# The low half of a split weight tile: 4,096 bytes behind its high half in place of 4,224

## The chip, the cores and the metric

The kernel runs on one core of a Trainium2 chip. Its time is device time in microseconds of one execution. Three runs of the kernel before took 1101.42, 1101.83 and 1102.53 us; the median, 1101.83 us, is what the changed kernel's median is set against.

## The reference

One layer of a hybrid encoder on 256 positions of 2,048 channels, float32 throughout. Cut to the products that carry the time:

```python
hn = rmsnorm(h, mix_norm_pre)
proj = hn @ w_in                       # 2048 -> 1024 (z) + 1536 (xbc) + 32 (dt) + 1024 (u)
y_ssd = ssd_mixer(z, xbc, dt_raw, ...) # convolution, two chunked scans, gate, norm
y_pool = pool_mixer(u, pool_w, pool_scale)
h = h + rmsnorm(concatenate([y_ssd, y_pool]) @ w_out, mix_norm_post)   # 2048 -> 2048
hn = rmsnorm(h, ffn_norm_pre)
gate, val = split(hn @ w_ffn_up)       # 2048 -> 2 x 5632
ff = (gelu(dwconv_centred(gate, ...)) * val) @ w_ffn_down              # 5632 -> 2048
h = h + rmsnorm(ff, ffn_norm_post)
gate = sigmoid(rmsnorm(h, ple_norm_pre) @ w_ple_gate)                  # 2048 -> 2048
h = h + rmsnorm(gate * (p @ w_ple), ple_norm_post)                     # 256 -> 2048
```

## The kernel before, in words

**Split operands.** TensorE multiplies in a rounded 32-bit format (float32r). To keep float32 accuracy every operand is held as a high half, the value rounded to that format, and a low half, the rounded remainder. A product x w is then three matmuls: high x with high w, high x with low w, low x with high w. `split` makes the two halves of a weight: ScalarE copies the raw tile into the high half (line 195), VectorE subtracts that from the raw tile into the low half (line 196).

**Where the halves lie.** `weight_pair` takes one tile of 2,112 float32 columns (8,448 bytes in each partition) from a ring of five, and gives its first 1,056 columns to the high half and the rest to the low one. Only the first product, dtu, has 1,056 columns to a tile; all other weights come in pieces of 1,024 or 512 columns, which begin at the start of each half. Some weight tiles of the gate product do not come from the ring: they are given pages (tiles of 8,192 bytes, tag "pg"; names gth, gtl, gtfh, gtfl), high and low in pages of their own. Activations (hn, wox, cath, catl, dnxh, dnxl) lie in pages too; the split parts of the hidden layer (hs, hd) lie in tiles of 1,024 columns, high in front, low 512 columns behind.

**Three kinds of product use a weight tile.**

- `seven_products` and, for the output projection, `units` with `products`: two blocks of rows at once by a scheme of seven block products in place of eight. Tiles named a, b, c and d hold sums of weight blocks. For each block product the weight is the moving operand, 512 columns, in the order xh wh, xh wl, xl wh, into one bank: 21 matmuls for a unit (lines 341 and 1076). The lists WO_FAST (2 and 4 units), dn_fast (19 and 16) and gt_fast (3 and 3) say which units go this way.
- `token_major` and `units` otherwise: the weight is again the moving operand, 512 columns; for one stationary operand there are two matmuls, to two banks, and the order is xh wh twice, xh wl twice, xl wh twice (lines 398 and 1138). z, part of the output projection (woa), of the down product (dna), of the gate product (gt) and the embedding (ple) are done so.
- `feature_pairs`: the weight is the stationary operand, 128 columns, and the activation moves. For each weight slice there is a matmul of the high weights with 512 columns (high and low activation side by side) and one of the low weights with 256 (lines 414 and 415). xbc and the up projection (ga, va) are done so.

The stages follow each other: dtu up to 51 us, xbc to 136, z to 190, the output projection to 280, the up projection from 286 to 778, the down product to about 1003, the gate product to 1091. Weights stream in from HBM through queues of SyncE; block sums of weights are written back to HBM by GpSimd's queue and read again. The order of the instructions on ScalarE, VectorE and SyncE is recorded as it is written (`in_order`) and kept.

Of the kernel before, what the change touches and what calls it, by code (L numbers as in the profile page):

```python
# [86 lines left out]
def build(nc, a, out):  # L87
# [6 lines left out]
    with tile.TileContext(nc) as tc, \  # L94
# [82 lines left out]

        def weight_pair(name):
            w = wp.tile([P, 2112], F32R, tag="w", bufs=5, name=f"{name}w")
            return w[:, :1056], w[:, 1056:]  # L180

        def split(name, src, nel, cuts=()):

            if name in ready:
                return ready.pop(name)
            if name in spare:
                hi, lo = spare.pop(name)
            else:
                hi, lo = weight_pair(name)
            for c0, c1 in zip((0, *cuts), (*cuts, nel)):  # L190
                s = slice(c0, c1)
                v = src[:, s] if name != "dtu0" else r0[:, W_0[c0 // 352]:W_0[c0 // 352] + 352]
                if (name, c0) == ("dtu0", 0):
                    continue
                last["act"] = ins(nc.scalar.copy(hi[:, s], v))
                last["dve"] = ins(nc.vector.tensor_sub(lo[:, s], v, hi[:, s].bitcast(F32)))
            return hi, lo
# [279 lines left out]
        def first_panel(t):  # L477
            c = (V_SCW, W_0[1] - P)[t]
            return put([v[:, t * P:(t + 1) * P] for v in hn(0)], r0[:, c:c + P], r0[:, V_MIX:V_MIX + 1])

        spare["dtu0"] = weight_pair("dtu0")
        turned = ins(nc.vector.tensor_copy(spare["dtu0"][0][:, :352], r0[:, W_0[0]:W_0[0] + 352]))
        with tc.issue_after(turned):
# [870 lines left out]
        for i, w_ in enumerate(which[2:] + which[:2]):  # L1354
            fetch, add, store = block_sums(*w_, i >= len(which) - 2)
            n = 45 * i // 10 + 4
# [379 lines left out]
```

## Time and profile before

| | before |
|---|---|
| median of 3 runs | 1101.83 us (1101.42 to 1102.53) |
| the profiled execution's own time | 1101.12 us |
| its span, first to last instruction | 1099.3 us |
| mean granted TensorE clock | 0.999 |
| TensorE busy | 1093.2 us, 99% |
| VectorE busy | 976.7 us, 89% |
| ScalarE busy | 738.3 us, 67% |
| HBM traffic | 343 GB/s over the span |

Times in the profile's rows are microseconds, durations of one instruction nanoseconds. A row of the groups reads: line, engine, operation, written tile, read tiles, shape, count, then busy time and mean duration of one, then the engine's idle time before them and what ended it. A row of the timeline gives the start, the time taken and the engine, then the same; instructions of one kind that follow each other are merged, with their number behind the x. For a matmul the first of the tiles read that comes from a weight tile carries its name (dn_0w, gt08bw); the row does not say whether the high or the low half was read, so this is taken from the order in the code. The ends of matmuls are modelled; their starts are not.

### The profile page before, as it was taken

To read this page: it belongs to the slowest core of one execution; us is meant where nothing else is said; L and a number is where in the kernel's file an instruction comes from. 1 tells how busy PE (TensorE), PEld (TensorE's weight loads), DVE (VectorE), ACT (ScalarE), POOL (GpSimd) and SP (SyncE) were. 2 spreads that over 40 slices of the span, in tenths; PEclk is the share of its full clock that TensorE was granted. 3 is DMA by queue.
4 is the path that set the end of the run, shared out by engine and by line. 5 is a ranking of instruction groups with operands and counts; after the bars stand their busy time and mean duration, and the time that the engine had idled before them with its cause. 6 is when DMAs were issued, how large, how long until landed. Compare 5 with 4: busy or idle time off the path is not lost.

```text
span 1099.3 us, 15720 instructions
## 1 busy us (share of the span) xinstructions
PE 1093.2 (99%) x5766; PEld 936.8 (85%) x5766; DVE 976.7 (89%) x1367; ACT 738.3 (67%) x1109; POOL 98.8 (9%) x163
## 2 busy tenths in 40 slices
PE   9999999999999999999999999999999999999998
PEld 9988888888888888888888888888888888888886
DVE  6679988999879888889889988888999999999997
ACT  6687777566775565565756646657688878776773
POOL 0211101100100000000000000000000000051001
PEclk9999999999999999999999999999999999999999
DMA  9987699587589999999999998999999999995872
GB/s 361 423 253 208 193 273 277 211 323 267 186 343 402 395 403 368 393 360 364 385 370 379 366 391 346 401 364 421 356 411 382 370 350 385 418 380 226 312 276 77
DMA packets 59565, 367.45 MB, mean 334 GB/s; under 512 B 6672, under 2 KB 7696, under 8 KB 24208
## 3 DMA queue, kind: packets, MB, share of 16 engines
q1 hardware_dynamic: 45808, 302.74, 70.4%
q0 software_dynamic: 13536, 63.44, 17.3%
q8 instruction: 45, 0.74, 0.2%
q14 instruction: 32, 0.26, 0.1%
q10 hardware_dynamic: 144, 0.26, 0.1%
HBM read 315.56 MB, written 61.34 MB: 343 GB/s over the span
## 4 chain that ended last, share of the span: by engine, by line
PE 97%; DVE 1%; POOL 1%; ACT 0%; issue 0%; POOLq 0%; DVEq 0%; ACTq 0%
PE ga L123 22%; PE va L123 22%; PE dna L123 11%; PE xbc L123 6%; PE woa L123 5%; PE gt L123 5%; PE dns L123 4%; PE dtu L123 4%; PE z L123 4%; PE dn0s L123 2%; PE dn1s L123 2%; PE ple L123 1%; PE wo1s L123 1%; PE gts L123 1%; PE yd L123 1%; PE pw L123 1%
## 5 line engine op out<-in xcount | busy, mean ns | idle before, releaser
L123 PE MATMUL ga<-wox,ug_0w 128*128 128x512 f32 x704 | 130.8, 337 | 0.0
L123 PE MATMUL ga<-wox,ug_1w 128*128 128x512 f32 x704 | 130.1, 337 | 0.0
L123 PE MATMUL va<-wox,uv_1w 128*128 128x512 f32 x704 | 129.2, 337 | 0.0
L123 PE MATMUL va<-wox,uv_0w 128*128 128x512 f32 x704 | 129.2, 337 | 0.0
L123 PEld LDWEIGHTS ga<-wox,ug_0w 128*128 128x128 f32 x704 | 107.6, 188 | 14.5 <-ACT pl L1288 0.2
L123 PEld LDWEIGHTS va<-wox,uv_1w 128*128 128x128 f32 x704 | 107.5, 188 | 14.5
L123 PEld LDWEIGHTS va<-wox,uv_0w 128*128 128x128 f32 x704 | 107.5, 188 | 14.5
L123 PEld LDWEIGHTS ga<-wox,ug_1w 128*128 128x128 f32 x704 | 107.5, 188 | 14.5 <-DVE wox L233 0.2
L304 DVE TENSOR_TENSOR dnb<-dnb 128x512 f32<-128x512 f32 x128 | 88.2, 689 | 3.0
L282 POOL DMA_DIRECT2D dns<-dnb x30 | 16.1, 536 | 317.1 <-DVE dnb L304 266.0
L1205 ACT CAST he<-he 128x512 fp32r<-128x512 f32 x13 | 8.1, 621 | 42.7 <-DVE he L1204 42.7
L123 PE MATMUL xbc<-hn,xb_1w 128*128 128x512 f32 x192 | 36.5, 338 | 0.0
L123 PE MATMUL xbc<-hn,xb_0w 128*128 128x512 f32 (+1 forms) x192 | 36.5, 340 | 0.0
L123 PEld LDWEIGHTS xbc<-hn,xb_0w 128*128 128x128 f32 x192 | 29.7, 188 | 4.1
L123 PEld LDWEIGHTS xbc<-hn,xb_1w 128*128 128x128 f32 x192 | 29.5, 188 | 4.1 <-issue 0.2
L1368 ACT CAST hs<-hid 128x384 fp32r<-128x384 f32 (+1 forms) x44 | 23.4, 537 | 13.6 <-PE dna L123 13.4
L1448 ACT ACTIVATE fc<-gr,vt 128x256 f32<-128x256 f32 x44 | 26.1, 593 | 9.0 <-DVE gr L1441 9.0
L1520 POOL DMA_DIRECT2D hd<-hsum x24 | 12.7, 529 | 193.0 <-PE dn0s L123 70.5
L123 PE MATMUL dna<-dn_0w,hs 128*128 128x512 f32 x108 | 28.6, 394 | 0.0
L123 PE MATMUL dna<-dn_1w,hs 128*128 128x512 f32 x108 | 28.2, 392 | 0.0
L1369 DVE TENSOR_TENSOR hs<-hid,hs 128x384 fp32r<-128x384 f32 (+1 forms) x44 | 25.4, 580 | 2.6 <-ACT hs L1368 2.6
L1451 DVE TENSOR_TENSOR fc<-fc,ft 128x510 f32<-128x510 f32 x22 | 15.1, 689 | 11.3 <-ACT ft L1449 11.3
(1778 smaller groups left out, 2796.8 us busy)
## 6 DMA issues: line engine op xcount, KB each, us to landing
dnb<-w_down SPq DMA_DIRECT2D x32, 1024.0 KB, 10.6
dns<-dnb POOLq DMA_DIRECT2D x30, 1024.0 KB, 7.6
hd<-hsum POOLq DMA_DIRECT2D x24, 512.0 KB, 8.3
dtur<-w_dtu SPq DMA_DIRECT2D x14, 528.0 KB, 9.8
hsum<-he POOLq DMA_DIRECT2D x13, 512.0 KB, 8.0
gtb<-w_gate SPq DMA_DIRECT2D x6, 1024.0 KB, 10.5
gts<-gtb POOLq DMA_DIRECT2D x6, 1024.0 KB, 9.5
dn1r<-w_down SPq DMA_DIRECT2D x6, 1024.0 KB, 7.8
```

What stands on the lines that cost most here:

```text
L123: last["pe"] = ins(nc.tensor.matmul(o, lhsT, rhs, start=start, stop=stop, skip_group_check=True))
L282: nc.gpsimd.dma_start(t, pg[0])
L304: nc.vector.tensor_add(s[:, i], v[:, i], a[:, b])
L1205: nc.scalar.copy(o[:, :512], s[:, :512])
L1368: nc.scalar.copy(t[:, :c1], hid_part(k)[:, :c1])
L1369: nc.vector.tensor_sub(t[:, 512:512 + c1], hid_part(k)[:, :c1], t[:, :c1].bitcast(F32))
L1448: nc.scalar.activation(c[:, f], v[:, f], AF.Identity, bias=vec(V_FCB + 4 * s + 2 * i + f), scale=vec(w + NF))
L1451: nc.vector.tensor_add(c[:, :, 1:], c[:, :, 1:], l[:, :, :L - 1])
L1520: nc.gpsimd.dma_start(o.bitcast(F32), kept[k])
```

## The change

The high half keeps its place. The low half begins right behind the 1,024th column, 4,096 bytes behind the high half's start, and the tile's last 64 columns stay empty. Tiles of the first product (names that begin with dtu) keep 1,056 columns to a half, 4,224 bytes. The tile's size, the ring and all other tiles are as before, and so are the number, the kind and the order of the instructions on every engine.

```diff
         def weight_pair(name):
             w = wp.tile([P, 2112], F32R, tag="w", bufs=5, name=f"{name}w")
-            return w[:, :1056], w[:, 1056:]
+            n = 1056 if name.startswith("dtu") else 1024
+            return w[:, :n], w[:, n:2 * n]
```

## The prediction

> **What bounds the kernel now.** I read the page first: busy time per engine, then the chain that ended last.
>
> ```profile
> span 1099.3 us, 15720 instructions
> PE 1093.2 (99%) x5766; PEld 936.8 (85%) x5766; DVE 976.7 (89%) x1367; ACT 738.3 (67%) x1109; POOL 98.8 (9%) x163
> PE 97%; DVE 1%; POOL 1%; ACT 0%; issue 0%; POOLq 0%; DVEq 0%; ACTq 0%
> ```
>
> TensorE is busy 99% of the span and is 97% of the chain. What it waits for is almost nothing: the view of waits for PE holds two rows.
>
> ```profile
> PE dtu L140 <- DVE ones L138: 1.0, 1, 1.0
> PE mx L123 <- DVE mixl L767: 0.2, 1, 0.2
> ```
>
> So the time is the number of matmuls times the distance from one matmul's start to the next. A matmul's listed duration is modelled and overlaps the next one's; the distance is not in the groups, but the timeline gives starts, and a merged row's start less the start before it, divided by the matmuls between, is the spacing. The question of this case is whether the spacing depends on where an operand lies.
>
> The change moves no instruction: order and number are the same on all five engines, and every tile keeps its address. Tiles of the page, hs and weight pools all begin at remainder 96 when the address is divided by 256 (as the built program places them), and a slice of 512 columns is 2,048 bytes long, a multiple of 256. So in the products that carry the time every moving operand has remainder 96, except one kind: a low half 4,224 = 16 x 256 + 128 bytes behind its high half, remainder 224. The change gives it 4,096 = 16 x 256, remainder 96 like the rest.
>
> **Part 1, the seven-product units** (line 123, called from line 341 and, for the output projection, from line 1076; xh with wh, xh with wl, xl with wh, so every third moving operand is a low half). TensorE's timeline in the gate product:
>
> ```profile
> 1029.18 0.62 PE L123 MATMUL gt<-gt08bw,dnxh 128*128 128x512 f32 x2
> 1029.64 0.39 PE L123 MATMUL gt<-gt08bw,dnxl 128*128 128x512 f32 x1
> 1029.87 0.62 PE L123 MATMUL gt<-gt08dw,dnxh 128*128 128x512 f32 x2
> ...
> 1038.79 0.62 PE L123 MATMUL gt<-gt012bw,dnxh 128*128 128x512 f32 x2
> ```
>
> From 1029.18 to 1038.79 lie two units, 42 matmuls, in 9.61 us: 228.8 ns each. Inside a triple, high and low together take 0.46 us and the third matmul 0.23. The same order of three, with weights that lie in two page tiles (high and low both at remainder 96), stands later in the same product:
>
> ```profile
> 1068.35 0.39 PE L123 MATMUL gt<-gth,dnxh 128*128 128x512 f32 x1
> 1068.57 0.39 PE L123 MATMUL gt<-gtl,dnxh 128*128 128x512 f32 x1
> 1068.80 0.39 PE L123 MATMUL gt<-gth,dnxl 128*128 128x512 f32 x1
> ...
> 1071.07 0.69 PE L123 MATMUL gt<-gth,dnxh 128*128 128x512 f32 x2
> ```
>
> Twelve matmuls in 2.72 us: 226.7 ns each, the low ones 0.23 like the others. Two units at that spacing would be 42 x 0.2267 = 9.52 us, so a unit is 0.045 us too long, 6.4 ns for each of its seven low halves. The code has 47 such units (lists WO_FAST with 2 + 4, dn_fast with 19 + 16, gt_fast with 3 + 3): 47 x 0.045 = **2.1 us**. Is it load, not place, since few other engines work at 1068? In the busy down product the unit is the same:
>
> ```profile
> 822.65 0.85 PE L123 MATMUL dna<-dn018bw,hs 128*128 128x512 f32 x3
> 827.46 0.85 PE L123 MATMUL dna<-dn020bw,hs 128*128 128x512 f32 x3
> ```
>
> 21 matmuls in 4.81 us, 229.0 ns each. What costs the 6.4 ns, remainder 224 itself or the jump from 96 to 224 and back, makes no difference to the sum, since the change ends both.
>
> **Part 2, the regular products** (lines 398 and 1138: pairs of matmuls to two banks share a stationary operand; two of six move a low half).
>
> ```profile
> 1018.83 1.08 PE L123 MATMUL gt<-gt_0w,dnxh 128*128 128x512 f32 x4
> 1027.11 1.08 PE L123 MATMUL gt<-gt_1w,dnxh 128*128 128x512 f32 x4
> ```
>
> Here 36 matmuls took 8.28 us: 230.0 ns, 3.3 above the aligned 226.7. How many there are:
>
> ```profile
> L123 PE MATMUL dna<-dn_0w,hs 128*128 128x512 f32 x108 | 28.6, 394 | 0.0
> L123 PE MATMUL z<-z_1w,hn 128*128 128x512 f32 x96 | 24.6, 394 | 0.0
> L123 PE MATMUL woa<-wo_0w,cath 128*128 128x512 f32 x80 | 22.5, 395 | 0.0
> L123 PE MATMUL woa<-wo_0w,catl 128*128 128x512 f32 x40 | 13.5, 395 | 0.0
> L123 PE MATMUL gt<-gt_0w,dnxh 128*128 128x512 f32 x52 | 15.2, 392 | 0.0
> ```
>
> The 394 here is the modelled duration, not the spacing; only the counts are used. With the tiles of the other number: dna 216, z 192, woa 240, gt 104 and half as many again with dnxl, 156. The embedding's 48 I leave out. Whether all 3.3 ns go is open, since an aligned stretch just after an interruption is slow too:
>
> ```profile
> 1073.05 0.39 PE L123 MATMUL gt<-gth,dnxh 128*128 128x512 f32 x1
> 1073.97 0.39 PE L123 MATMUL gt<-gtl,dnxh 128*128 128x512 f32 x1
> ```
>
> Four in 0.92 us, 230.0 ns with nothing at 224. The bounds are therefore nothing and (216 + 192 + 240 + 156) x 3.3 = 2.7 us. I take all of it in dna and gt, 372 x 3.3 = 1.2 us, which run long without other matmuls between, and a third in z and woa, which are broken up by the mixer's small ones: 432 x 3.3 / 3 = 0.5. Together **1.7 us**.
>
> **Part 3, the feature products** (lines 414 and 415, xbc and the up projection), the longest stage. Here the weight tiles are stationary; the moving operand is a page, at 96 always. What moves is the load of the low weights.
>
> ```profile
> 600.48 2.94 PE L123 MATMUL ga<-wox,ug_0w 128*128 128x512 f32 x16
> 603.26 2.94 PE L123 MATMUL ga<-wox,ug_1w 128*128 128x512 f32 x16
> 606.03 2.94 PE L123 MATMUL ga<-wox,ug_0w 128*128 128x512 f32 x16
> ```
>
> From 600.48 to 606.03 lie 32 matmuls, 16 of 512 and 16 of 256 columns, in 5.55 us: 346.9 ns a pair. The first product, which the change leaves as it is, reads thirds of 352 columns:
>
> ```profile
> 39.72 3.05 PE L123 MATMUL dtu<-dtu12w,hn 128*128 128x352 f32 x18
> 42.60 3.05 PE L123 MATMUL dtu<-dtu13w,hn 128*128 128x352 f32 x18
> ```
>
> 18 in 2.88 us, 160.0 ns. With the aligned 226.7 at 512 that is a slope of 66.7 / 160 = 0.417 ns a column and 13.3 ns a matmul; a pair of 512 and 256 is then 226.7 + 120.0 = 346.7. The pairs are at it. Nothing is lost here, so nothing can come back: **0**, with a bound of 0.2 ns x 1,600 pairs (1,408 of the up projection, 192 of xbc, by the code's loops) = 0.3 us faster. The loss is priced under the rivals.
>
> The Trainium skill, "TensorE: Matmul & The Clock Gate", sections "Step-by-step: what each phase is for" and "Back-to-back issue gap", gives TensorE two independent read ports and a spacing of N / 2.4 + 2.5 ns, 215.8 ns at 512 columns, with no term for an address. By it the sum of this change would be zero. The trace disagrees with the figure (226.7 at best) and, by the two stretches of part 1, with there being no such term.
>
> **Part 4, the engines that fill the tiles.** Lines 195 and 196 write the two halves.
>
> ```profile
> L196 DVE TENSOR_TENSOR dn_1w<-dn1r,dn_1w 128x1024 fp32r<-128x1024 f32 x6 | 7.3, 1215 | 0.0
> L196 DVE TENSOR_TENSOR gtl<-gt1r,gth 128x1024 fp32r<-128x1024 f32 x4 | 4.8, 1218 | 0.0
> L195 ACT CAST dn_1w<-dn1r 128x1024 fp32r<-128x1024 f32 x6 | 6.3, 1052 | 2.8 <-PE dna L123 2.8
> L195 ACT CAST gth<-gt1r 128x1024 fp32r<-128x1024 f32 x4 | 4.0, 1054 | 0.0
> ```
>
> With both halves at 96 (gth, gtl) they take 3 and 2 ns more than 128 bytes apart: nothing. What a faster TensorE asks of them, by the table of stretches (span; PE, PEld, DVE, ACT and POOL; the granted clock, the DMA share, GB/s):
>
> ```profile
> 800.00:985.00 185.00, 185.00 (x805) 150.65 (x804) 178.83 (x211) 149.36 (x189) 25.08 (x22) 1.00 0.97 384
> ```
>
> VectorE has 6.2 us free in 185, and the saving there is about 2 us; it stays hidden unless the free time sits in the wrong places.
>
> **Sum.** 2.1 + 1.7 = 3.8 us. The profiled execution took 1101.12 us around its span of 1099.3; it would be 1097.3, the span 1095.5. The median of the runs is 0.71 us higher, so I forecast 1101.83 - 3.8 = **1098.0 us**. Its own range, from 0 to 2.7 in part 2, with 0.25 for the timeline's rounding in part 1 and 0.3 in part 3, is 1096.5 to 1100.0.
>
> **The rivals.**
> (a) *Place is not the cause*: the second moving read of one stationary operand costs the 6.4 ns whatever its address, or a distance of 4,096 does what 4,224 does. Then the time stays at 1101.8. For it: only a few clean triples are aligned. Against it: these have the same order and none of the 6.4 ns. 13%. The rule of the Trainium skill in part 3 ("TensorE: Matmul & The Clock Gate") leads to this time too.
> (b) *Supply takes the place*: in the down product VectorE (178.83 of 185) or the DMA queues (0.97 busy there) hold TensorE to today's pace. Then what dna gives is lost, 35 units x 0.045 + 216 x 3.3 ns = 2.3 us, and 1.5 remain: 1100.3. Against it: TensorE never waits there now. 9%.
> (c) *The low weight load collides* (the other side): in the feature products the load of the low half now falls on the remainder that the moving stream reads. If each of 1,600 loads then cost what a misplaced low half costs, 3 x (228.8 - 226.7) = 6.3 ns, that is 10.1 us, less the 3.8: 1108.1. It turns the balance from 2.4 ns a pair on. For it: no pair there has its low weights at 96 today. Against it: in the aligned triples load and stream share the remainder and run at the best spacing. 8%.
>
> **How the numbers follow.** The forecast has 70%. Under 0.2% (2.2 us) this kernel cannot be told from no change; of the forecast's range some 4 in 70 lie there. Faster: 0.66. Within: 0.04 + 0.13 + 0.09 = 0.26. Slower: 0.08. The range runs from 1095.8 (all bounds on the good side, and the embedding) to 1101.6, which takes in (b) and nearly half of (a).
>
> **What would show it.** Right: units of 4.76 us in the timeline of the down and gate products, low and high matmuls 0.23 apart; the regular stretch near 227 ns; 346.9 ns a pair unchanged in the up projection. Wrong: units still at 4.81 (a); new waits of PE on ACT, DVE or DMA between 780 and 1000 (b); pairs over 349 ns (c).

## The result, and the profile after

The changed kernel took 1106.79 us (median of 6 runs, 1106.43 to 1107.55) against 1102.03 us (6 runs): a ratio of 1.0042, 95% interval 1.0032 to 1.0052. It is slower by 0.42%; the forecast was 1098.0 us, 0.35% faster. In the timed comparisons below, single executions stand 5 to 7 us above the rest, three of the kernel before (1107.59, 1108.67, 1108.85) and one of a kernel here called split (1102.24); none of them was profiled, so their cause stays open.

The page of the changed kernel, the span, the busy times and the chain by engine:

```profile
span 1105.8 us, 15720 instructions
PE 1098.6 (99%) x5766; PEld 938.2 (85%) x5766; DVE 977.0 (88%) x1367; ACT 740.1 (67%) x1109; POOL 100.2 (9%) x163
PE 91%; DMA 3%; DVE 3%; ACT 1%; POOL 1%; issue 1%; POOLq 0%; DVEq 0%; SPq 0%; ACTq 0%
```

TensorE still sets the end, with the same number of instructions, and is busy 5.4 us longer. So single matmuls stand further apart, somewhere. In TensorE's timeline of the up projection a row is one piece of weights, 16 matmuls in 8 pairs:

```profile
607.84 3.00 PE L123 MATMUL ga<-wox,ug_1w 128*128 128x512 f32 x16
610.67 2.98 PE L123 MATMUL ga<-wox,ug_0w 128*128 128x512 f32 x16
613.49 2.88 PE L123 MATMUL ga<-wox,ug_1w 128*128 128x512 f32 x15
```

16 pairs in 5.65 us, 353.1 ns a pair where the kernel before had 346.9. The gate product went the way that was forecast. Its regular part, then two units of seven products:

```profile
1025.83 1.07 PE L123 MATMUL gt<-gt_0w,dnxh 128*128 128x512 f32 x4
...
1032.63 1.07 PE L123 MATMUL gt<-gt_1w,dnxh 128*128 128x512 f32 x4
...
1036.03 0.62 PE L123 MATMUL gt<-gt08bw,dnxh 128*128 128x512 f32 x2
1036.48 0.39 PE L123 MATMUL gt<-gt08bw,dnxl 128*128 128x512 f32 x1
1036.71 0.62 PE L123 MATMUL gt<-gt08dw,dnxh 128*128 128x512 f32 x2
...
1045.55 0.62 PE L123 MATMUL gt<-gt012bw,dnxh 128*128 128x512 f32 x2
```

Thirty regular matmuls took 6.80 us, 226.7 ns each (before: 230.0), and two units 9.52 us, 4.76 each (before: 4.805); a high and a low matmul together now take 0.45 where they took 0.46. In the down product TensorE met two waits that it did not have before (view of waits):

```profile
PE dna L123 <- ACT dn126dw L196: 0.6, 1, 0.6
PE dns L123 <- DVE dn126aw L197: 0.3, 1, 0.3
```

The stages, from the start of each one's first matmul to the start of the next one's (the first: from the start of the span; the last: to its end), in us. The first stage, which no kernel here touches, differed from the kernel before by up to 0.6 among them.

| stage | before | after | difference | split kernel, difference |
|---|---|---|---|---|
| first product | 51.67 | 51.81 | +0.14 | -0.45 |
| xbc | 84.89 | 85.14 | +0.25 | +0.01 |
| z | 54.08 | 53.42 | -0.66 | -0.64 |
| output projection | 95.62 | 94.67 | -0.95 | -0.89 |
| up projection | 491.72 | 500.89 | +9.17 | +0.05 |
| down product | 225.60 | 224.75 | -0.85 | -1.75 |
| gate product to the end | 95.77 | 95.11 | -0.66 | -0.66 |

The products whose weights move gained 3.1 us, those whose weights are stationary lost 9.4.

### The profile page after: what moved, and what is told of

It is laid out like the page before. It is cut to its first block, busy times and chain, and to the rows that moved or that the text cites. A ratio compares the mean times of both kernels' runs of the same rounds, so it can differ in the third digit from the quotient of the medians.

```text
span 1105.8 us, 15720 instructions
## 1 busy us (share of the span) xinstructions
PE 1098.6 (99%) x5766; PEld 938.2 (85%) x5766; DVE 977.0 (88%) x1367; ACT 740.1 (67%) x1109; POOL 100.2 (9%) x163
## 4 chain that ended last, share of the span: by engine, by line
PE 91%; DMA 3%; DVE 3%; ACT 1%; POOL 1%; issue 1%; POOLq 0%; DVEq 0%; SPq 0%; ACTq 0%
PE ga L123 23%; PE va L123 22%; PE dna L123 8%; PE woa L123 5%; PE gt L123 5%; PE xbc L123 5%; PE dtu L123 4%; PE z L123 4%; PE dns L123 3%; PE dn0s L123 2%; DMA dn126r<-w_down 1%; DMA dn114t<-dns 1%; PE ple L123 1%; PE wo1s L123 1%; DMA dn1r<-w_down 1%; PE dn1s L123 1%
## 5 line engine op out<-in xcount | busy, mean ns | idle before, releaser
L123 PE MATMUL ga<-wox,ug_1w 128*128 128x512 f32 x704 | 132.4, 340 | 0.0
L123 PE MATMUL va<-wox,uv_1w 128*128 128x512 f32 x704 | 131.6, 340 | 0.0
L123 PE MATMUL va<-wox,uv_0w 128*128 128x512 f32 x704 | 131.6, 340 | 0.0
L421 ACT COPY hid<-va 128x256 f32<-128x256 f32 x44 | 15.5, 372 | 16.6 <-PE va L123 16.6
```

Of the source, the lines that this page charges most:

```text
L123: last["pe"] = ins(nc.tensor.matmul(o, lhsT, rhs, start=start, stop=stop, skip_group_check=True))
L421: nc.scalar.copy(o[:, f * L:(f + 1) * L], acc[f][:, L:])
```

## Taking the change apart

All kernels below differ from the kernel before in `weight_pair` alone, unless a diff says more. A tile is written (high, low) by the columns at which its halves begin; a column is 4 bytes, and the first product keeps (0, 1056) throughout. "Feature tiles" are those of xbc and the up projection (names with xb, ug, uv), "moving tiles" all others.

**The split kernel: each kind of tile its own distance.**

```diff
-            return w[:, :1056], w[:, 1056:]
+            hi, lo, n = (0, 1056, 1056) if name.startswith("dtu") else \
+                (0, 1056, 1024) if name.startswith(("xb", "ug", "uv")) else (0, 1024, 1024)
+            return w[:, hi:hi + n], w[:, lo:lo + n]
```

> The low half lies 4,224 bytes behind the high half in the tiles of xbc and the up projection (there the weights are stationary), 4,096 in all others but the first product's. If the loss of the change lies in the feature products alone (353.3 ns a pair of matmuls in the changed kernel's timeline, 346.9 before, 1,600 pairs) and the gain in the products whose weights move (227 ns in place of 229 to 231), the two come apart: pairs at 346.9, units of the down product at 4.76 us, and a time of about 1102.0 - 3 = 1099. If the slower feature products only shift waits (a supply that is late whatever TensorE does), the time stays near 1105 to 1107. If the down product is held by its supply, the gain shrinks to about 1 and the time is near 1101.

Measured: 1097.29 us (median of 11) against 1102.32 (16), ratio 0.9957, 95% interval 0.9945 to 0.9969. Its up projection in the timeline:

```profile
606.88 2.94 PE L123 MATMUL ga<-wox,ug_1w 128*128 128x512 f32 x16
609.65 2.94 PE L123 MATMUL ga<-wox,ug_0w 128*128 128x512 f32 x16
612.43 2.94 PE L123 MATMUL ga<-wox,ug_1w 128*128 128x512 f32 x16
```

16 pairs in 5.55 us, 346.9 ns. The gain of the moving tiles stands alone now, and the last column of the table gives it by stage: 3.9 us over z, output projection, down and gate product. It beats both kernels.

**The other half of the split.** Feature tiles (0, 1024), moving tiles (0, 1056).

> The reverse: 4,096 in the tiles of xbc and the up projection alone, 4,224 in all others. If the feature products carry the loss by themselves: 353.3 ns a pair, and 1102.0 + 1,600 x 6.4 ns = 1112. If the loss comes from the moving tiles or from both together, the time is at or under 1107 and the pairs are at 346.9.

Measured: 1110.92 us. The same view of this kernel:

```profile
606.83 3.00 PE L123 MATMUL ga<-wox,ug_0w 128*128 128x512 f32 x16
609.66 3.00 PE L123 MATMUL ga<-wox,ug_1w 128*128 128x512 f32 x16
612.49 2.98 PE L123 MATMUL ga<-wox,ug_0w 128*128 128x512 f32 x16
```

5.66 us for 16 pairs, 353.8 ns by these two-digit starts; the up projection as a whole is 9.15 us longer than before, the other stages within 0.3. The loss belongs to the feature tiles, the gain to the moving tiles, and they add up.

## Which feature of the place decides

**Feature tiles, 4,352 bytes apart.** Feature tiles (0, 1088), moving tiles (0, 1024).

> As the split kernel, but the low half of the tiles of xbc and the up projection lies 4,352 bytes behind the high half: 17 x 256, so the remainder by 256 is that of 4,096 and the distance is not. If the remainder decides (load and moving stream both at 96): 353.3 ns a pair, 1099 + 10 = 1109. If the distance of 4,096 decides: 346.9 a pair, about 1099.

Measured: 1098.09 us. The up projection took 491.80 us, as before the change, though the low half has the remainder 96 by 256 again. That spoke for the distance and against the remainder.

**Feature tiles, both halves shifted by 128 bytes.** Feature tiles (32, 1056), moving tiles (0, 1024).

> As the split kernel, but in the tiles of xbc and the up projection the high half begins 128 bytes into the tile and the low half 4,096 behind it: both loads at remainder 224, the moving stream at 96. If a load is dear because it has the stream's remainder: 346.9 a pair, about 1099. If a load is dear because it has the remainder of the load before it (high and low alike): 353.3 a pair, about 1109.

Measured: 1103.89 us, the up projection 6.08 us longer than before. Its timeline:

```profile
605.97 2.98 PE L123 MATMUL ga<-wox,ug_1w 128*128 128x512 f32 x16
608.79 2.97 PE L123 MATMUL ga<-wox,ug_0w 128*128 128x512 f32 x16
611.59 2.97 PE L123 MATMUL ga<-wox,ug_1w 128*128 128x512 f32 x16
614.40 1.80 PE L123 MATMUL ga<-wox,ug_0w 128*128 128x512 f32 x9
```

24 pairs in 8.43 us: 351.2 ns, neither of the two values that were expected. Both theories miss.

**Feature tiles, high and low exchanged in remainder.** Feature tiles (32, 1088), 4,224 bytes apart, moving tiles (0, 1024).

> As the split kernel, but in the tiles of xbc and the up projection the high half lies at remainder 224 and the low half at 96 by 256, 4,224 bytes apart. If the distance between the two halves decides: 346.7 a pair, about 1097.5. If the low load's remainder against the moving stream's decides (both 96, as in the changed kernel): 353 a pair, about 1107.

Measured: 1104.73 us, the up projection 7.32 us longer, 352.0 ns a pair. At a distance of 4,224 this should have been fast if the distance decided; it lies near the value for the remainder, and is not that either.

**One distance for all, 4,352.** Feature tiles and moving tiles (0, 1088).

> One distance for all tiles but the first product's: 4,352 = 17 x 256 bytes. The feature products are fast with it (346.8 a pair, shown). For the tiles whose weights move: if the remainder by 256 decides: units 4.76, time about 1097.5, the gain of the split with one number. If the remainder by 512 decides there (4,352 leaves 256): units about 4.81 as with 4,224, time about 1101 to 1102.

Measured: 1107.32 us. The moving tiles did what a rule by 256 asks, units of 4.76 us in the gate product. But the feature tiles, the very same (0, 1088) in the same places as in the kernel at 1098.09, were slow. The two timelines, first with moving tiles (0, 1024):

```profile
608.14 2.94 PE L123 MATMUL ga<-wox,ug_1w 128*128 128x512 f32 x16
610.92 2.94 PE L123 MATMUL ga<-wox,ug_0w 128*128 128x512 f32 x16
613.69 2.47 PE L123 MATMUL ga<-wox,ug_1w 128*128 128x512 f32 x13
```

and with moving tiles (0, 1088):

```profile
608.14 3.00 PE L123 MATMUL ga<-wox,ug_1w 128*128 128x512 f32 x16
610.97 2.98 PE L123 MATMUL ga<-wox,ug_0w 128*128 128x512 f32 x16
613.79 2.52 PE L123 MATMUL ga<-wox,ug_1w 128*128 128x512 f32 x13
```

5.55 us against 5.65 for 16 pairs, with identical feature tiles. No rule on the place of these tiles alone can give that. (The two ran on different chips; the interruptions below show both spacings within one execution.) Pair by pair, the starts in the trace, in ns, show what differs: in the slow kernel the spacings repeat as 350, 361, 349 ns for the whole up projection behind its first 20 us, in the fast one as 347, 347, 346. In xbc, which has the mixer's small matmuls between its own, the slow kernels change between 350, 361, 349 and a fast 350, 343; each holds until the next such matmul or wait. That gave a new theory, tested below: a repeating pattern is started by whatever interrupted the stream last, and then keeps itself; the place of the halves only decides which patterns exist.

**Feature tiles, 4,160 bytes apart.** Feature tiles (0, 1040), moving tiles (0, 1024).

> As the split kernel, but the low half of the tiles of xbc and the up projection lies 4,160 bytes behind the high half (4,096 + 64). 4,224 and 4,352 gave 346.7 and 346.8 ns a pair, 4,096 gave 353.3. If only loads at the very same remainder by 512 are slow: 346.7 a pair, about 1097.5. If loads are slow as long as they lie within the same 128-byte piece of 512: 353, about 1107; anything between says that it is graded.

Measured: 1098.22 us, 346.7 ns a pair: 64 bytes off is fast, at least by the pattern that this kernel entered.

**Moving tiles, both halves at 224.** Feature tiles (0, 1056), moving tiles (32, 1056).

> As the split kernel (1097.3, units 4.76, regular products near 227 ns), but in the tiles whose weights move, the high half begins 128 bytes into the tile and the low half 4,096 behind it: both at remainder 224 by 256, the stationary operands at 96. If the jump from one half's remainder to the other's costs (no jump here): units 4.76, about 1097. If a moving operand at 224 costs because the stationary ones lie at 96: every one of some 1,840 matmuls pays up to 6.4 ns, units up to 4.90, time up to 1109.

Measured: 1105.51 us. One unit of the gate product in this kernel:

```profile
1037.56 0.63 PE L123 MATMUL gt<-gt010bw,dnxh 128*128 128x512 f32 x2
...
1042.47 0.63 PE L123 MATMUL gt<-gt012bw,dnxh 128*128 128x512 f32 x2
```

21 matmuls in 4.91 us, 233.8 ns: all are slow, the high ones too, though there is no jump between them. So in these products moving operands at 224 cost even where there is no jump. The prediction had left open whether 224 itself or the jump costs, and its sum held for either. Whether 224 is dear because the stationary operands lie at 96, or whatever their place, no kernel here can tell: none moved the stationary operands of these products.

## Interrupting the stream on purpose

To start the pattern often, TensorE got extra 128-column transposes, one to four of them, before a piece of the up projection at 20 places. The pieces hold 8 pairs and the places lie 8 pieces apart, so a stretch has 64 pairs; the "32 pairs" of the expectation was a slip, its sums are not touched by it.

```diff
+                if n >= 16 and n % 8 == 0:
+                    if n == 16:
+                        slab["idle"] = misc("idleu")
+                    with tc.issue_after(last["pe"]):
+                        for _ in range(n // 8 % 4 + 1):
+                            last["pe"] = ins(nc.tensor.transpose(slab["idle"][:, :P], ident, ident))
```

> The changed kernel (4,096 everywhere but in the first product) with one to four 128-column transposes between the feature products of the up projection, at 20 places, 32 pairs apart: 50 extra matmuls of about 0.11 us, 5.5 us, whose result is not used. If the distance alone sets the spacing, each stretch returns to 353.3 ns a pair and the time is near 1106.8 + 5.5 = 1112. If the spacing is a repeating pattern that the last interruption starts and that then keeps itself (4,352 gave 346.8 in one kernel and 353.3 in another with the same feature tiles), stretches of 32 pairs differ: some at 353.3 (350, 361, 349 in turn), some at 346.7 (350, 343 in turn, seen in short stretches of xbc), and the time lies between 1103 and 1112.

Measured: 1111.40 us. Two neighbouring stretches, the pieces in the middle of each left out:

```profile
382.45 2.94 PE L123 MATMUL ga<-wox,ug_1w 128*128 128x512 f32 x16
...
399.09 2.94 PE L123 MATMUL ga<-wox,ug_1w 128*128 128x512 f32 x16
401.87 0.38 PE L1481 MATMUL idleu<-ident 128*128 128x128 f32 x2
402.00 3.07 PE L123 MATMUL va<-wox,uv_0w 128*128 128x512 f32 x16
404.91 2.99 PE L123 MATMUL va<-wox,uv_1w 128*128 128x512 f32 x16
...
421.87 3.00 PE L123 MATMUL va<-wox,uv_1w 128*128 128x512 f32 x16
```

48 pairs from 382.45 to 399.09: 16.64 us, 346.7 ns. Then two transposes, and 48 pairs from 404.91 to 421.87: 16.96 us, 353.3 ns. The same tiles at 4,096 bytes run at the best spacing or at the worst, and change only at an interruption. Of the 21 stretches 5 were fast. Each of the five followed one or four transposes, never two or three; but five others behind one or four were slow, so the number alone does not decide, and what does was not found.

> The split kernel (4,224 in the tiles of xbc and the up projection, 4,096 in the others) with the same transposes at the same 20 places. If the distance alone sets the spacing: 346.7 a pair in every stretch, 1097.3 + 5.5 = about 1103. If interruptions start the pattern: stretches at 350 (352, 348 in turn, seen in xbc) beside some at 346.7, up to 1097.3 + 5.5 + 1,280 x 3.3 ns = 1107.

Measured: 1105.70 us. The same interruptions with feature tiles at 4,224:

```profile
381.73 2.96 PE L123 MATMUL ga<-wox,ug_1w 128*128 128x512 f32 x16
...
398.53 2.96 PE L123 MATMUL ga<-wox,ug_1w 128*128 128x512 f32 x16
401.33 0.38 PE L1481 MATMUL idleu<-ident 128*128 128x128 f32 x2
...
404.32 2.94 PE L123 MATMUL va<-wox,uv_1w 128*128 128x512 f32 x16
...
420.96 2.94 PE L123 MATMUL va<-wox,uv_1w 128*128 128x512 f32 x16
```

16.80 us for 48 pairs, 350.0 ns, and after the next interruption 16.64, 346.7. So 4,224 has a slow pattern too, milder (348, 352 or 349, 351 in turn), and 11 of the 21 stretches took it. The profiled execution of the kernel before did not, in its up projection: it entered the fast one after the last small matmuls, at 306 us, and kept it.

**Four interruptions, then none**, in the changed kernel (the condition is `16 <= n <= 40 and n % 8 == 0`).

> The changed kernel with transposes before the feature products at four places only (3, 4, 1 and 2 of them, at the first four of the 20 places), and none after. With 20 places the stretch after the fourth took the fast pattern. If the pattern keeps itself until it is interrupted, the rest of the up projection (136 pieces of 8 pairs, 1,088 pairs) stays at 346.7 ns a pair: 1106.8 - 1,088 x 6.6 ns + 10 x 0.11 us = about 1100.7. If the slow pattern comes back by itself: 353.3 and about 1108.

Measured: 1106.26 us. The expectation had miscounted: with 20 places the fast stretch had followed the third interruption, and the fourth was followed by a slow one. This kernel repeated both, fast after the third (346.8), slow after the fourth; it differs in the stretch ahead of the first interruption, fast here and slow there, with the same tiles. So the predicted gain did not come, but the pattern did keep itself: the slow one ran for 1,087 pairs, to the end of the up projection, without a change. From the late part:

```profile
740.91 3.00 PE L123 MATMUL ga<-wox,ug_0w 128*128 128x512 f32 x16
...
752.22 3.00 PE L123 MATMUL ga<-wox,ug_0w 128*128 128x512 f32 x16
```

32 pairs in 11.31 us, 353.4 ns. What was not shown is a kernel at 4,096 that enters the fast pattern and keeps it to the end; that the loss would then be gone is argued from the fast stretches.

**Is there a distance without a slow pattern?** The split kernel with 4,160 and with 4,288 in the feature tiles, and the 20 interruptions.

> The split kernel with 4,160 in the tiles of xbc and the up projection, and transposes at the 20 places. If 4,160 has no slow pattern: 346.7 a pair in all stretches, 1098.2 + 5.5 = about 1103.5. If it has one (353, 354 in turn were seen in two short stretches of xbc): some stretches at 353, up to 1098.2 + 5.5 + 1,280 x 6.6 ns = 1112.

Measured: 1102.63 us. All 21 stretches were fast; after some interruptions two or three pairs took 353 to 357 ns, and the stream then fell back to 346.7 by itself. The two stretches at the same places as above:

```profile
381.14 2.94 PE L123 MATMUL ga<-wox,ug_1w 128*128 128x512 f32 x16
...
397.78 2.94 PE L123 MATMUL ga<-wox,ug_1w 128*128 128x512 f32 x16
400.56 0.38 PE L1481 MATMUL idleu<-ident 128*128 128x128 f32 x2
...
403.56 2.94 PE L123 MATMUL va<-wox,uv_1w 128*128 128x512 f32 x16
...
420.20 2.94 PE L123 MATMUL va<-wox,uv_1w 128*128 128x512 f32 x16
```

That is not the same as having no slow pattern. In xbc, all three kernels with 4,160 hold the slow spacing (353, 353, 354 ns) through one whole run of 16 pairs and over seven pairs of the next. In this one:

```profile
118.12 2.99 PE L123 MATMUL xbc<-hn,xb_0w 128*128 128x512 f32 x16
120.94 2.99 PE L123 MATMUL xbc<-hn,xb_1w 128*128 128x512 f32 x16
123.77 0.62 PE L123 MATMUL seg<-seg_x,seg_w 128*128 128x512 f32 x2
```

16 pairs in 5.65 us, 353.1 ns. So 4,160 has a slow pattern too; none of the 20 interruptions started one that lasted.

> The same with 4,288 (4,096 + 192). If the relation by 256 decides and is symmetrical, as 4,160: the same stretches. If a distance of 192 has no slow pattern: 346.7 in all stretches, about 1103.

Measured: 1105.89 us. 11 stretches fast, 10 at 350 (354 and 346, or 355 and 345, in turn): as with 4,224, and not as with 4,160.

**4,160, timed.** Feature tiles (0, 1040), moving tiles (0, 1024), as above.

> 4,160 in the tiles of xbc and the up projection, 4,096 in the others, timed. If 4,160 has no slow pattern: all executions within 1096.5 to 1098.5, ratio about 0.996, the up projection at 346.7 ns a pair. If single slow executions have another cause than the pattern, some stand 4 to 5 us higher here too.

Measured: 1097.18 us (median of 7, 1096.55 to 1097.88) against 1101.97 (12), ratio 0.9946, 95% interval 0.9923 to 0.9969. It is as fast as the split kernel, and with the 20 interruptions its up projection was 2.1 us shorter than that kernel's (497.5 against 499.7). All seven executions lie in the range that was expected without a slow pattern in the up projection.

## Why the prediction was wrong, point by point

- **Bound and wording of the change: right.** TensorE's spacing set the time before and after, and nothing but the place of the low half moved.
- **Part 1, seven-product units: right.** Forecast 4.76 us in place of 4.805, measured 4.76 in the gate product. Low and high matmuls are alike in the changed kernel.
- **Part 2, regular products: right, and sized low.** Forecast 1.7 us of at most 2.7. In the gate product the spacing went to 226.7 in full. In z and the output projection a third of 3.3 ns a matmul was taken, and nearly all of it came: z gave 0.66 us where 192 x 3.3 ns are 0.63, the output projection 0.95 where 240 x 3.3 ns and six units are 1.06. Parts 1 and 2 together were put at 3.8 us; the split kernel measured 3.9, the changed one 3.1.
- **Part 4 and rival (b): a part of it came.** The down product gave 0.85 us in the changed kernel and 1.75 in the split, against the 2.3 of rival (b)'s sum, with waits of 0.6 and 0.3 us on ScalarE and VectorE that were not there before. Across the kernels with moving tiles at 96 it gave 0.3 to 2.4. The starts in the trace show where the rest went: add up by how much each distance of over 245 ns between two starts exceeds 227 ns, and the stage holds 0.6 us of such gaps before, 1.5 in the split kernel and 2.4 in the changed one. In each of the 13 kernels with moving tiles at 96, the gain and the growth of the gaps together come to 2.6 to 2.8 us. So the closer spacing came in full everywhere, and gaps took 0.3 to 2.4 us of it back; why they differ from kernel to kernel stays open.
- **Part 3, feature products: this is the step that failed.** It said that nothing is lost there and set the term to 0; the first half was right (346.7 is the best that any kernel here reached), and the second was taken for the whole. Rival (c), which names the loss, got 8%, because "in the aligned triples load and stream share the remainder and run at the best spacing". That argument carried a finding from a product of 512 columns throughout to one where 512 and 256 alternate, and there it does not hold. Measured in the changed kernel: 9.2 us in the up projection and 0.25 in xbc, 353.3 ns a pair, where (c) was priced at 10.1. The mechanism of (c) is not right either: it is not each low load that costs 6.3 ns, but a pattern of three pairs that costs 20 ns and that the same tiles may or may not enter. That its price came near is luck. The slope of part 3 also took the first product's 352-column matmuls for undisturbed ones. They are not: a third of 352 columns is 1,408 = 5 x 256 + 128 bytes, so 8 of the 18 moving operands of a tile begin at 224. Their starts give 160.5 ns a matmul (mean of eight tiles), where 226.7 at 512 columns and 120.0 at 256 make 160.0 at 352: the slope came out right only because 224 costs some 1 ns in this form, by an estimate from these numbers, and not 6.4.
- **What the trace of before could have told.** Its xbc stage, between the small matmuls, has stretches at 348, 352 beside stretches at 346.7 with tiles of the same geometry:

```profile
54.53 2.94 PE L123 MATMUL xbc<-hn,xb_1w 128*128 128x512 f32 x16
57.30 2.02 PE L123 MATMUL mx<-pmat,u 128*128 128x136 f32 x16
...
79.90 2.96 PE L123 MATMUL xbc<-hn,xb_0w 128*128 128x512 f32 x16
82.70 1.09 PE L123 MATMUL mx<-pmat,u 128*128 128x136 f32 x8
```

Eight pairs took 2.77 us in the first place, 346 ns a pair, and 2.80 in the second, 350. That two spacings exist for one geometry was there to be seen; only the clean middle of the up projection was read.

## What to carry to other kernels

Where TensorE is the bound, measure the start-to-start spacing of its matmuls per product form, from the timeline and not from the listed durations, and hold it against the best spacing that the same form reaches anywhere in the trace; the place of an operand in SBUF is then worth a sweep, for moving and stationary tiles apart, since one distance helped one form and hurt the other. One fast stretch does not prove the geometry: interrupt the stream on purpose before trusting it, and prefer a distance at which it comes back to the fast spacing (here 4,160 bytes for the stationary tiles, in all 21 stretches of the up projection though not everywhere in xbc; for the moving tiles 4,096).

## What the runs showed of the hardware

- Matmuls of 512 moving float32r columns stood 226.7 ns apart when moving and stationary operands all lay at remainder 96 by 256 bytes, and 233.8 when all moving operands lay at 224 (one unit of the gate product). At 352 columns, with 8 of 18 moving operands at 224, the mean was 160.5, 0.5 ns above what 226.7 at 512 and 346.7 for a pair of 512 and 256 give.
- A stream of 512 and 256 columns in turn, with its low weights 4,096 bytes behind the high ones, repeats 350, 361, 349 ns or 350, 343 ns a pair; at 4,224 bytes 347, 347, 346 or 348, 352; at 4,288 346.7 on average or 354, 346; at 4,160 346.7 on average throughout the up projection, but 353, 353, 354 in a run of xbc. One or two transposes of 128 columns were enough to change from one to the other, and 1,087 pairs in a row kept what they had.
- The Trainium skill, "SBUF — State Buffer", section "Who interferes with whom", gives TensorE one read port for the moving operand and an independent one for the weights. By that alone the place of the weights would not matter to the matmuls; here moving nothing but that place changes their spacing by up to 6.6 ns a pair (353.3 against 346.7). Whether the load then delays the moving stream or one load the next was not shown.
